# Down projection of a decoder step: second parts a slot later, one bank in two tiles, loads two pairs ahead, one sum by an adding transfer

## The chip, the cores and the metric

The kernel runs on one core of one Trainium2 chip. The metric is the device time of one execution in microseconds, as the median of three runs. Engines are named as in the profile: PE (matrix multiplies, with PEld for its weight loads), DVE (vector work), ACT (copies and activations), POOL, and SP, which issues most of the transfers. A row that ends in "q" (SPq, POOLq) is a transfer being issued by that engine.

## The reference, cut

One layer of a hybrid decoder is computed for 512 prompt rows and 64 sample rows (576 in all), in float32. The change lies in the last stage, the down projection of the gated feed-forward net:

```python
D_MODEL = 2048
D_FF = 5632
def _conv_ffn(x, prev, p):
    u = _rms(x, p['g_ffn']) @ p['w_up']
    up = jnp.concatenate([prev, u], axis=1)
    c = p['conv_b'] + p['conv_w'][CONV_W - 1] * up[:, CONV_W - 1:]
    ...
    a, b = jnp.split(c, 2, axis=-1)
    return x + (jax.nn.silu(a) * b) @ p['w_down'], up[:, T:]
```

So the stage adds `g @ w_down` to `x`, where `g` has 5632 features and the result 2048.

## The kernel before

Float32 operands are split into a first part (`whi`, written by ACT) and a second part (`wlo` = value minus first part, written by DVE), and every product is three passes on PE: first by first, first by second, second by first. The passes come in that order, so a `wlo` is read only in the last third of its product.

The feed-forward's `g` is made tile by tile (44 tiles of 128 features) and kept in device memory as `gd`. The last of the 44 tiles is finished by `convolve(43, i)`, five pieces of DVE and ACT work, before `down` begins.

`down` has two parts. A plain one takes the first 512 of the 5632 features: 16 output tiles `ot`, each 24 matmuls of 128x128 by 288 columns into a `zp` tile, then one DVE addition to the sum `hT`. Then come 40 **pairs** n (5 groups of 1024 features, called chunks here, by 8 pairs of output tiles). A pair is a 2x2 block product done in seven products instead of eight, in the order P1, P6, P5, P7, P2, P3, P4; product number t = 7n + i, and I call the time of product i **slot** i. A product is 12 matmuls (3 passes of 4). It needs weights and activations that are sums of blocks. The weight sums are made per pair: S1 = A21 + A22, S2 = S1 - A11, S3 = A22 - S2, S4 = A12 - S2 (`down_sum`, one DVE operation of 128x512 each). The activation sums T1 to T4 are made once per chunk for the next one (`build`: 13 steps in `todo`, one taken in slot 3 and one in slot 6 of all pairs but the first of a chunk; no steps in the last chunk).

Three banks hold results: P1 and P2 go to `Z[0]`, P6, P7 and P4 to `Z[1]`, P5 and P3 to `Z[2]`. After each product one DVE operation of 128x288 adds its bank to the sums (`down_evict`), and the next product into that bank may start only then.

The order of the work is the order of the code: `down_first(t)` is the ACT copy, `down_second(t)` the DVE difference, `down_product(t)` the matmuls. Before, slot t holds: the first part for t+2, the eviction of t-1, the second part for t+2, a sum if one is due (S3 in slot 0, S4 in slot 2, S1 in slot 4, S2 in slot 5), a step of `todo`, the loads for pair n+1 (slot 1), and product t. Each engine works through its own queue in that order. SP's queue holds the loads (A21 and A22 into two 256 KB tiles of the pool `z` with 8 buffers, A11 and A12 together as one 512 KB tile `raw` with 2 buffers) and, in the last chunk, the stores of y. In the last chunk `store_y` also puts ten PE transposes into each pair, which use the free `fa` banks (4 in all, one of them held as `Z[2]`).

In the trace every instruction has line L189, that of a recording helper, so work is told by its tiles: `hT<-zp` or `hT<-fa` is an eviction, `wlo<-` a second part, `a<-a,a` is S1, `s<-a,raw` S2, `raw<-a,s` S3, `s<-raw,s` S4, and T1 to T4, B11, B21, B22 and `t` belong to `build`. On PE, a product is named by its activations: B11 is P1, T2 is P6, T1 is P5, T3 is P7, B21 is P2, B22 is P3 and T4 is P4.

Of the kernel before, what the change touches and what calls it, by code (L numbers as in the profile page):

```python
# [9 lines left out]
F32 = mybir.dt.float32  # L10
# [3 lines left out]
ALU = mybir.AluOpType  # L14
# [6 lines left out]
HB = 288  # L21
# [257 lines left out]
class Kern:  # L279
# [1910 lines left out]
    def down_weights(self, n, part):  # L2190

        if n >= 40:
            return
        r, c = 512 + 1024 * (n // 8), 256 * (n % 8) + 128 * part
        src = self.w_down[r:r + 1024, c:c + 128].rearrange("(k p) c -> p k c", p=128)
        if part == 0:
            t = self.wpool.tile([128, 8, 128], F32, name="raw", tag="raw", bufs=2)
            self.nc.sync.dma_start(out=t, in_=src)
            self.V[n, "A11"], self.V[n, "A12"] = t[:, :4], t[:, 4:]
        else:  # L2200
            for k in range(2):
                t = self.V[n, f"A2{k + 1}"] = self.vblock(f"a2{k + 1}")
                self.nc.sync.dma_start(out=t, in_=src[:, 4 * k:4 * k + 4])

    def vblock(self, name):
        return self.z(name)[:, :512].rearrange("p (k c) -> p k c", k=4)
# [211 lines left out]
    def finish(self, es, outs, w_down):  # L2418
        nc, a = self.nc, self.a
        self.fpool = self.pool(es, "ffn", side="right")  # L2420
        self.bpool = self.pool(es, "big", side="right")
        self.spawn(self.ffn_consts())
        self.cst, self.ssq, self.W = [None, None], None, {}
        self.B = {name: [[self.operand(name, n, half) for half in range(2)] for n in "hl"]
                  for _, name, _ in self.PRODUCTS.values()}
        order = [o for i in range(8) for o in (i, i + 8)]

        def xload(n):
            if n < 16:
                x = self.z("xr")  # L2430
                nc.sync.dma_start(out=x, in_=self.xT[order[n]])
                return x

        def free(kt):
            if kt == 0:
                self.weights(0, "A11")
                self.weights(0, "A22")
            elif kt in (1, 2):
                self.weights(0, ("A12", "A21")[kt - 1])
            elif kt == 6:  # L2440
                self.U = [self.place(12 + s, (128, FW), "u") for s in range(2)]
                for U in self.U:
                    nc.gpsimd.memset(U[:, 0:2], 0.0)
            elif kt == 7:
                self.C = [self.place(14 + s, (128, FW - 2), "C") for s in range(2)]
                self.first_parts(0, 0)
                self.second_parts()

        def later(kt):
            if kt == 4 and self.rest:  # L2450
                self.rest()
                self.rest = None

        x, self.rest = xload(0), None
        for n, ot in enumerate(order):
            last = n == 15
            ps, = self.gemm([(outs[ot], 128, list(range(8)), self.mixs)],
                            on_kt=lambda kt: (later(kt), last and free(kt)), before=self.mixed)
            nx = xload(n + 1)
            self.out_done(ot, ps, x)  # L2460
            x = nx
        self.rest()
        norm = self.spawn(self.second_norm(), first=True)
        self.Z = [self.zp(), self.zp(), self.ps("fa")]
        self.held.add(self.Z[2].tensor.name)
        self.gs, self.hT = [], {}
        self.gd = self.dram("gd", (128, 44, NT))
        self.st = Stream(self, 2, 4)
        downs = self.add_down(w_down, 0)
        self.w_down = w_down  # L2470
        win = a["win_sample"].rearrange("l b t k g d -> (l b) t (k g d)")
        todo = []
        for f in range(44):
            for i in range(7):
                if f == 0 and i == 3:
                    self.until(lambda: norm.done and not self.threads)
                parts = self.before_slot(f, i)
                if i > 3 and todo:
                    todo.pop(0)()
                self.product(f, i, parts)  # L2480
                if f == 43 and i in (0, 1):
                    todo += self.load_first(i)
            if 2 <= f < 18:
                b, t = (f - 2) // 2, 252 * (f % 2)
                nc.gpsimd.dma_start(out=win[b, t:t + 252],
                                    in_=a["cache_win"][0, b, 8 + t:260 + t].rearrange("t k g d -> t (k g d)"))
        while todo:
            todo.pop(0)()
        self.evict(43, 6)
        for i in range(5):  # L2490
            self.convolve(43, i)
        self.done(self.Z[2])
        self.down(downs)
        self.drain()

    def down(self, downs):
        for ot in range(2):
            self.load_h(ot)
        self.V, self.vs = {}, {}
        Y4 = self.fpool.tile([128, 4, HB], F32, name="Y4", tag="prev")  # L2500
        Y1 = self.fpool.tile([128, HB], F32, name="Y1", tag="cw")
        self.Y = [Y4[:, i] for i in range(4)] + [self.rstd[:, :HB], self.rstd[:, HB:], Y1]
        todo, B = self.build(1)
        for ot in range(16):
            hi, lo = self.st.get(downs[ot])
            o = self.zp()
            for kt in range(4):
                for n, (w, x) in enumerate(((hi, 0), (lo, 0), (hi, 1))):
                    for h in range(2):
                        self.mm(o[:, 512 * h:512 * h + HB], w[:, kt], self.gs[h][x][:, kt],  # L2510
                                kt == 0 and n == 0, kt == 3 and n == 2)
                    if n < 2:
                        self.pump()
            self.st.prep_to(downs[ot] + 5)
            h = self.h2(self.hT[ot])
            self.nc.vector.tensor_tensor(h, self.halves(o), h, ALU.add)
            if ot + 2 < 16:
                self.load_h(ot + 2)
            if 0 < ot < 15:
                todo.pop(0)()  # L2520
            if ot == 11:
                self.down_weights(0, 1)
            elif ot == 13:
                self.down_weights(0, 0)
            elif ot == 14:
                self.down_sum(0, "S1")
                self.down_first(0)
                self.down_sum(0, "S2")
                self.down_second(0)
                self.down_first(1)  # L2530
        self.down_second(1)
        self.Z = [self.zp(), self.zp(), self.ps("fa")]
        self.held.add(self.Z[2].tensor.name)
        for t in range(280):
            n, i = t // 7, t % 7
            if t % 56 == 0 and t:
                B = nextB
            if t % 56 == 0 and t < 224:
                todo, nextB = self.build(2 + t // 56)
            self.down_first(t + 2)  # L2540
            if t:
                self.down_evict(t - 1)
            self.down_second(t + 2)
            for m, name in {0: ((n, "S3"),), 2: ((n, "S4"),), 4: ((n + 1, "S1"),), 5: ((n + 1, "S2"),)}.get(i, ()):
                self.down_sum(m, name)
            if n % 8 and i in (3, 6) and todo:
                todo.pop(0)()
            if i == 1:
                self.down_weights(n + 1, 1)
                self.down_weights(n + 1, 0)  # L2550
            self.down_product(t, B)
        self.down_evict(279)

# [75 lines left out]
```

## Time and profile before

| | |
|---|---|
| median of three runs | 2978.86 us (2977.79 to 2979.95) |
| the profiled execution | 2977.68 us, of which 2975.9 us span |
| PE / DVE / ACT / POOL busy, share of the span | 97% / 75% / 49% / 13% |
| first product of pair 0, first product of pair 33, end | 2435.15, 2884.36, 2975.9 us |
| granted PE clock over the whole run | 0.993 |

The profile is of one execution; stretches are given in microseconds from the span's start. A view called windows gives the busy time of each engine in a stretch, a timeline lists instructions in order, and a view of waits adds up what an engine stood idle for. A granted clock of 1.00 is 2.4 GHz and one of 0.50 is 1.2 GHz. Busy time of DVE counts each operation to its last write, while the next may start some 0.08 us earlier, so durations in a row are a little longer than the distance of two starts.

### The profile page before, as it was taken

What the parts mean: (1) busy time and instruction counts of PE and PEld (TensorE: products, weight loads), DVE (VectorE), ACT (ScalarE), POOL (GpSimd) and SP (SyncE); (2) the same over time, 40 slices, a digit from 0 to 9 for tenths busy, and PEclk for the clock granted to TensorE, in tenths of its full rate; (3) what the DMA queues carried; (4) which work ended last, traced back from release to release, by engine and by line L of the source; (5) the groups of instructions that cost most, each with busy time, mean ns of one, the idle gap of its engine ahead of it and who ended that gap; (6) DMA issues with size and microseconds to landing.
All of it is one profiled execution on the core that took longest, in us unless ns stands there. A gap on an engine that the chain in (4) does not pass through costs nothing.

```text
span 2975.9 us, 56967 instructions
## 1 busy us (share of the span) xinstructions
PE 2880.6 (97%) x21370; PEld 2839.7 (95%) x21370; DVE 2221.1 (75%) x4403; ACT 1459.3 (49%) x2863; POOL 390.3 (13%) x681
## 2 busy tenths in 40 slices
PE   8999999999999999999999999999999998888889
PEld 7999999999999999999999999999999998888889
DVE  4332456766476566468999999999999978888888
ACT  6443568666354555334544454454454534333333
POOL 3011131312301111200111111111110100000000
PEclk9999999999999999999999999999999999999999
DMA  8443333222554566755444543433433452342333
GB/s 246 130 113 82 107 102 89 88 83 78 139 157 126 177 207 220 244 174 176 125 133 124 144 134 110 126 99 109 122 101 109 137 188 81 105 117 79 101 92 109
DMA packets 560143, 385.79 MB, mean 130 GB/s; under 512 B 65477, under 2 KB 527893, under 8 KB 559613
## 3 DMA queue, kind: packets, MB, share of 16 engines
q1 hardware_dynamic: 537068, 308.29, 36.5%
q0 software_dynamic: 22768, 73.86, 7.5%
q8 instruction: 169, 2.77, 0.4%
q14 instruction: 106, 0.86, 0.1%
q10 hardware_dynamic: 32, 0.01, 0.0%
HBM read 316.51 MB, written 75.32 MB: 132 GB/s over the span
## 4 chain that ended last, share of the span: by engine, by line
PE 54%; DVE 10%; issue 5%; ACT 3%; POOL 1%; DMA 0%; ACTq 0%; DVEq 0%; POOLq 0%
PE zp L189 39%; PE fa L189 15%; DVE wlo L189 3%; ACT whi L189 2%; DVE hT L189 1%; DVE s L189 1%; DVE t L189 1%; DVE a L189 1%; DVE raw L189 1%; POOL ret_sample L189 0%; DMA raw<-w_down 0%; DVE B22l L189 0%; POOL mix L189 0%; DVE T2l L189 0%; DVE B11l L189 0%
## 5 line engine op out<-in xcount | busy, mean ns | idle before, releaser
L189 ACT ACTIVATE whi<-raw 128x512 fp32r<-128x512 f32 x588 | 356.0, 625 | 460.7 <-PE zp L189 242.4
L189 DVE TENSOR_TENSOR wlo<-raw,whi 128x512 fp32r<-128x512 f32 x584 | 398.2, 697 | 118.7 <-ACT whi L189 116.1
L189 PE MATMUL zp<-ah,whi 128*128 128x288 f32 (+1 forms) x2208 | 480.9, 299 | 2.1 <-ACT whi L189 1.9
L189 PE MATMUL zp<-al,whi 128*128 128x288 f32 (+1 forms) x2208 | 478.1, 298 | 0.1
L189 PE MATMUL zp<-ah,wlo 128*128 128x288 f32 x2176 | 473.8, 299 | 3.1 <-DVE wlo L189 3.1
L189 ACT ACTIVATE whi<-s 128x512 fp32r<-128x512 f32 x256 | 156.3, 631 | 437.0 <-DVE s L189 343.9
L189 PEld LDWEIGHTS zp<-ah,whi 128*128 128x128 f32 (+1 forms) x2208 | 356.3, 189 | 5.5 <-ACT whi L189 2.3
L189 PEld LDWEIGHTS zp<-ah,wlo 128*128 128x128 f32 x2176 | 351.4, 189 | 6.4 <-DVE wlo L189 3.9
L189 PEld LDWEIGHTS zp<-al,whi 128*128 128x128 f32 (+1 forms) x2208 | 354.7, 188 | 1.8 <-DVE al L189 0.3
L189 ACT ACTIVATE whi<-a 128x512 fp32r<-128x512 f32 x344 | 202.2, 625 | 122.5 <-DVE u L189 78.2
L189 DVE TENSOR_TENSOR wlo<-a,whi 128x512 fp32r<-128x512 f32 x344 | 225.2, 687 | 29.0 <-ACT whi L189 26.2
L189 DVE TENSOR_TENSOR wlo<-s,whi 128x512 fp32r<-128x512 f32 x256 | 168.6, 687 | 28.2 <-ACT whi L189 28.2
L189 PE MATMUL zp<-T2h,whi 128*128 128x288 f32 x576 | 105.3, 301 | 51.5 <-DVE hT L189 51.4
L189 DVE SCALAR_TENSOR_TENSOR C<-u,cw,C 128x592 f32<-128x592 f32 x176 | 146.4, 832 | 3.1
L189 PEld LDWEIGHTS zp<-T2h,whi 128*128 128x128 f32 x576 | 84.4, 189 | 57.6 <-issue 30.5
L189 DVE CUSTOM_DVE_ANT_0 P<-fa,th 128x256 f32<-128x256 f32 (+3 forms) x128 | 60.9, 488 | 63.6 <-PE fa L189 61.7
L189 PE MATMUL zp<-T2h,wlo 128*128 128x288 f32 x576 | 103.4, 301 | 0.0
L189 PE MATMUL zp<-B11h,wlo 128*128 128x288 f32 x576 | 100.6, 294 | 2.3 <-DVE wlo L189 2.3
L189 PE MATMUL zp<-B11h,whi 128*128 128x288 f32 x576 | 100.3, 294 | 1.3 <-ACT whi L189 1.3
L189 DVE TENSOR_TENSOR hT<-zp,hT 128x288 f32<-128x288 f32 (+1 forms) x191 | 90.4, 478 | 14.5 <-PE zp L189 11.8
L189 PE MATMUL zp<-T2l,whi 128*128 128x288 f32 x576 | 101.2, 296 | 0.0
L189 PE MATMUL zp<-B11l,whi 128*128 128x288 f32 x576 | 100.2, 294 | 0.0
(435 smaller groups left out, 6640.1 us busy)
## 6 DMA issues: line engine op xcount, KB each, us to landing
a<-w_up SPq DMA_DIRECT2D x264, 256.0 KB
raw<-w_in SPq DMA_DIRECT2D x102, 512.0 KB
raw<-w_down SPq DMA_DIRECT2D x48, 512.0 KB
raw<-w_up SPq DMA_DIRECT2D x44, 512.0 KB
a<-w_down SPq DMA_DIRECT2D x80, 256.0 KB
raw<-w_out SPq DMA_DIRECT2D x32, 512.0 KB
gd<-g POOLq DMA_DIRECT2D x44, 288.0 KB, 2.9
xr<-xT SPq DMA_DIRECT2D x32, 288.0 KB
```

The costliest lines, as they stand in the source:

```text
L189: return fn(*a, **kw)
```

## The change

Five things change, all in and just before `down`.

1. `convolve(43, i)` moves from before `down` into the first two output tiles of its plain part (pieces 0 and 1 into the first, 2 to 4 into the second). The tiles `Y4` and `Y1`, which reuse memory of the convolution, are allocated after the plain part.
2. The second part is made a slot later: slot t makes it for t+1 instead of t+2. The first part stays two ahead. S2 moves from slot 5 to slot 6 and stands first there.
3. S1 is no DVE operation any more: A21 is loaded as before, and POOL issues a transfer that reads A22 from device memory and adds it to the tile of A21. A22 is still loaded by itself, too.
4. The weights of pair n+2 instead of n+1 are loaded, `raw` in slot 5 and the two others in slot 6.
5. `Z[1]` alternates between a `zp` tile and an `fa` tile from pair to pair. Two of the four `fa` banks are held then.

```diff
             for k in range(2):
                 t = self.V[n, f"A2{k + 1}"] = self.vblock(f"a2{k + 1}")
                 self.nc.sync.dma_start(out=t, in_=src[:, 4 * k:4 * k + 4])
+            t = self.V[n, "S1"] = self.V[n, "A21"]
+            self.nc.gpsimd.dma_start(out=t, in_=src[:, 4:], accum_op=ALU.add)
...
         self.evict(43, 6)
-        for i in range(5):
-            self.convolve(43, i)
...
             self.st.prep_to(downs[ot] + 5)
+            for i in ((0, 1), (2, 3, 4))[ot] if ot < 2 else ():
+                self.convolve(43, i)
...
-            if ot == 11:
-                self.down_weights(0, 1)
-            elif ot == 13:
-                self.down_weights(0, 0)
-            elif ot == 14:
-                self.down_sum(0, "S1")
-                self.down_first(0)
-                self.down_sum(0, "S2")
-                self.down_second(0)
-                self.down_first(1)
-        self.down_second(1)
-        self.Z = [self.zp(), self.zp(), self.ps("fa")]
-        self.held.add(self.Z[2].tensor.name)
+            if ot in (11, 12):
+                self.down_weights(ot - 11, 1)
+            elif ot in (13, 14):
+                self.down_weights(ot - 13, 0)
...
+        self.down_sum(0, "S2")
+        for t in range(2):
+            self.down_first(t)
+        self.down_second(0)
+        A, C = self.zp(), self.ps("fa")
+        self.held.add(C.tensor.name)
+        bs = self.zp(), self.ps("fa")
+        self.held.add(bs[1].tensor.name)
         for t in range(280):
...
+            if i == 6:
+                self.down_sum(n + 1, "S2")
             self.down_first(t + 2)
             if t:
                 self.down_evict(t - 1)
-            self.down_second(t + 2)
-            for m, name in {0: ((n, "S3"),), 2: ((n, "S4"),), 4: ((n + 1, "S1"),), 5: ((n + 1, "S2"),)}.get(i, ()):
+            if i == 0:
+                self.Z = [A, bs[n % 2], C]
+            self.down_second(t + 1)
+            for m, name in {0: ((n, "S3"),), 2: ((n, "S4"),)}.get(i, ()):
                 self.down_sum(m, name)
...
-            if i == 1:
-                self.down_weights(n + 1, 1)
-                self.down_weights(n + 1, 0)
+            if i == 5:
+                self.down_weights(n + 2, 0)
+            elif i == 6:
+                self.down_weights(n + 2, 1)
             self.down_product(t, B)
```

**DVE at the end of a pair.** These are DVE's rows from slot 4 of one pair to slot 0 of the next, in the first chunk, before:

```order
L189 TENSOR_TENSOR a_31324<-a_31324,a_31326 128x512
L189 TENSOR_TENSOR hT<-zp,hT 128x288
L189 TENSOR_TENSOR wlo<-raw,whi 128x512
L189 TENSOR_TENSOR s_31404<-a_31324,raw 128x512
L189 TENSOR_TENSOR hT<-fa,hT 128x288
L189 TENSOR_TENSOR wlo<-s_31404,whi 128x512
L189 TENSOR_TENSOR T2l<-t,T2h 128x576
L189 TENSOR_TENSOR t<-B21l,t 128x576
L189 TENSOR_TENSOR hT<-zp,hT 128x288
L189 TENSOR_TENSOR wlo<-a_31324,whi 128x512
L189 TENSOR_TENSOR raw<-a_31326,s_31404 128x512
```

And these are the rows of the changed kernel from slot 5 of that pair to slot 0 of the next one:

```order
L189 TENSOR_TENSOR hT<-zp,hT 128x288
L189 TENSOR_TENSOR wlo<-a_31155,whi 128x512
L189 TENSOR_TENSOR s_31417<-a_31290,raw 128x512
L189 TENSOR_TENSOR hT<-fa,hT 128x288
L189 TENSOR_TENSOR wlo<-raw,whi 128x512
L189 TENSOR_TENSOR T2l<-t,T2h 128x576
L189 TENSOR_TENSOR t<-B21l,t 128x576
L189 TENSOR_TENSOR hT<-zp,hT 128x288
L189 TENSOR_TENSOR wlo<-s_31417,whi 128x512
L189 TENSOR_TENSOR raw<-a_31292,s_31417 128x512
```

The row of S1 is gone, S2 stands in slot 6 ahead of the eviction of P3, and the second part that follows the same eviction is that of the product one earlier.

**PE's banks.** In one pair of two, P6, P7 and P4 write an `fa` tile; this is the difference at such a pair:

```order
 L189 MATMUL zp<-B11h,wlo 128x288 x4
-L189 MATMUL zp<-T2h,whi 128x288 x4
-L189 MATMUL zp<-T2l,whi 128x288 x4
-L189 MATMUL zp<-T2h,wlo 128x288 x4
+L189 MATMUL fa<-T2h,whi 128x288 x4
+L189 MATMUL fa<-T2l,whi 128x288 x4
+L189 MATMUL fa<-T2h,wlo 128x288 x4
 L189 MATMUL fa<-T1h,whi 128x288 x4
 L189 MATMUL fa<-T1l,whi 128x288 x4
 L189 MATMUL fa<-T1h,wlo 128x288 x4
```

The order of the products is unchanged; what P6 waits for is now the eviction of the P4 before last.

**DVE at the start of the pairs.** This is the difference after the last step of `build` in the plain part; the second row that stays is the addition of the last output tile:

```order
 L189 TENSOR_TENSOR B22l<-B22l,B22h 128x1152
-L189 TENSOR_TENSOR a_30885<-a_30885,a_30887 128x512
-L189 TENSOR_TENSOR s_30980<-a_30885,raw 128x512
-L189 TENSOR_TENSOR wlo<-raw,whi 128x512
 L189 TENSOR_TENSOR hT<-zp,hT 128x576
-L189 TENSOR_TENSOR wlo<-s_30980,whi 128x512
+L189 TENSOR_TENSOR s_31011<-a_30883,raw 128x512
+L189 TENSOR_TENSOR wlo<-raw,whi 128x512
+L189 TENSOR_TENSOR wlo<-s_31011,whi 128x512
```

S2 and the first second part of pair 0 now stand behind that addition.

## Rows read from the trace of the kernel before

**Rows 1.** Page, part 1: busy time and share of each engine.
```profile
PE 2880.6 (97%) x21370; PEld 2839.7 (95%) x21370; DVE 2221.1 (75%) x4403; ACT 1459.3 (49%) x2863; POOL 390.3 (13%) x681
```

**Rows 2.** Windows: length, busy PE, PEld, DVE, ACT, POOL, clock, DMA share, GB/s.
```profile
2435.00:2884.00 449.00, 389.70 (x2773) 380.27 (x2772) 377.87 (x676) 168.79 (x283) 0.00 (x0) 0.97 0.35 101
2884.00:2970.00 86.00, 86.00 (x665) 85.85 (x664) 75.78 (x157) 34.13 (x63) 0.00 (x0) 1.00 0.38 110
```

**Rows 3.** Waits from 2435 to 2884: us in total, times, longest.
```profile
DVE wlo L189 <- ACT whi L189: 63.6, 126, 1.6
PE zp L189 <- DVE hT L189: 57.9, 39, 2.6
```

**Rows 4.** Timeline of PE: first products of pairs 0, 17, 18, 33, 35, 36.
```profile
2435.15 0.69 PE L189 MATMUL zp<-B11h,whi 128*128 128x288 f32 x4
...
2666.49 0.69 PE L189 MATMUL zp<-B11h,whi 128*128 128x288 f32 x4
...
2677.59 0.69 PE L189 MATMUL zp<-B11h,whi 128*128 128x288 f32 x4
...
2884.36 0.69 PE L189 MATMUL zp<-B11h,whi 128*128 128x288 f32 x4
...
2908.77 0.69 PE L189 MATMUL zp<-B11h,whi 128*128 128x288 f32 x4
...
2920.98 0.69 PE L189 MATMUL zp<-B11h,whi 128*128 128x288 f32 x4
```

**Rows 5.** Timeline of DVE at the end of pair 5, then PE.
```profile
2515.68 0.69 DVE L189 TENSOR_TENSOR a<-a,a 128x512 f32<-128x512 f32 x1
2516.29 0.45 DVE L189 TENSOR_TENSOR hT<-zp,hT 128x288 f32<-128x288 f32 x1
2516.65 0.69 DVE L189 TENSOR_TENSOR wlo<-raw,whi 128x512 fp32r<-128x512 f32 x1
...
2518.72 0.69 DVE L189 TENSOR_TENSOR wlo<-s,whi 128x512 fp32r<-128x512 f32 x1 [0.41 <-ACT whi L189]
2519.33 0.75 DVE L189 TENSOR_TENSOR T2l<-t,T2h 128x576 fp32r<-128x576 f32 x1
2520.11 0.76 DVE L189 TENSOR_TENSOR t<-B21l,t 128x576 f32<-128x576 f32 x1
2520.79 0.45 DVE L189 TENSOR_TENSOR hT<-zp,hT 128x288 f32<-128x288 f32 x1
...
2521.39 0.37 PE L189 MATMUL zp<-T2h,whi 128*128 128x288 f32 x1 [2.60 <-DVE hT L189]
```

**Rows 6.** Windows behind another wait of PE, columns as above.
```profile
2574.00:2576.50 2.50, 2.50 (x13) 2.50 (x12) 2.09 (x5) 1.15 (x2) 0.00 (x0) 0.50 0.36 105
```

**Rows 7.** Timeline at the start of the plain part: DVE, then PE.
```profile
2382.20 3.31 DVE L189 SCALAR_TENSOR_TENSOR C<-u,cw,C 128x592 f32<-128x592 f32 x4
...
2387.09 0.40 PE L189 MATMUL zp<-B11h,wlo 128*128 128x288 f32 x1 [2.34 <-DVE wlo L189]
```

**Rows 8.** Timeline of DVE: the addition of the last output tile.
```profile
2436.03 0.75 DVE L189 TENSOR_TENSOR hT<-zp,hT 128x576 f32<-128x576 f32 x1
```

**Rows 9.** A load of A21: SP's timeline; windows of its bytes, and of A22 with `raw`.
```profile
2559.64 5.49 SPq L189 DMA_DIRECT2D a<-w_down  x2
...
2560.50:2562.00 1.50, 1.50 (x13) 1.50 (x12) 1.09 (x4) 0.98 (x2) 0.00 (x0) 1.00 0.59 174
2565.50:2569.00 3.50, 3.50 (x28) 3.50 (x28) 2.60 (x6) 1.66 (x3) 0.00 (x0) 1.00 0.81 229
```

**Rows 10.** Page, part 6: transfers issued by POOL: count, KB, us to landing.
```profile
al<-mix POOLq DMA_DIRECT2D x8, 288.0 KB, 4.8
xc<-xc POOLq DMA_DIRECT2D x4, 256.0 KB, 6.5
```

**Rows 11.** Timeline of DVE and POOL at the end of the stage before.
```profile
2375.25 1.35 DVE L189 TENSOR_TENSOR B11l<-B11l,B11h 128x1152 fp32r<-128x1152 f32 x1
2375.63 0.55 POOL L189 DMA_DIRECT2D gd<-g  x1 [4.19 <-DVE g L189]
2376.18 1.69 POOL L189 COPY u<-prev 128x16 f32<-128x16 f32 x1
```

More of the change, by code (lines that the diff above doesn't have):

```diff
@@ L2499, in down @@
         self.V, self.vs = {}, {}
-        Y4 = self.fpool.tile([128, 4, HB], F32, name="Y4", tag="prev")
-        Y1 = self.fpool.tile([128, HB], F32, name="Y1", tag="cw")
-        self.Y = [Y4[:, i] for i in range(4)] + [self.rstd[:, :HB], self.rstd[:, HB:], Y1]
         todo, B = self.build(1)
@@ L2520, in down @@
                 todo.pop(0)()
-            if ot == 11:
-                self.down_weights(0, 1)
-            elif ot == 13:
-                self.down_weights(0, 0)
-            elif ot == 14:
-                self.down_sum(0, "S1")
-                self.down_first(0)
-                self.down_sum(0, "S2")
-                self.down_second(0)
-                self.down_first(1)
-        self.down_second(1)
-        self.Z = [self.zp(), self.zp(), self.ps("fa")]
-        self.held.add(self.Z[2].tensor.name)
+            if ot in (11, 12):
+                self.down_weights(ot - 11, 1)
+            elif ot in (13, 14):
+                self.down_weights(ot - 13, 0)
+        Y4 = self.fpool.tile([128, 4, HB], F32, name="Y4", tag="prev")
+        Y1 = self.fpool.tile([128, HB], F32, name="Y1", tag="cw")
+        self.Y = [Y4[:, i] for i in range(4)] + [self.rstd[:, :HB], self.rstd[:, HB:], Y1]
+        self.down_sum(0, "S2")
[6 more added lines that the diff above has]
+        self.held.add(bs[1].tensor.name)
         for t in range(280):
@@ L2537, in down @@
                 B = nextB
-            if t % 56 == 0 and t < 224:
-                todo, nextB = self.build(2 + t // 56)
+            if i == 6:
+                self.down_sum(n + 1, "S2")
             self.down_first(t + 2)
@@ L2542, in down @@
                 self.down_evict(t - 1)
-            self.down_second(t + 2)
-            for m, name in {0: ((n, "S3"),), 2: ((n, "S4"),), 4: ((n + 1, "S1"),), 5: ((n + 1, "S2"),)}.get(i, ()):
+            if i == 0:
+                self.Z = [A, bs[n % 2], C]
+            self.down_second(t + 1)
+            for m, name in {0: ((n, "S3"),), 2: ((n, "S4"),)}.get(i, ()):
                 self.down_sum(m, name)
+            if t % 56 == 0 and t < 224:
+                todo, nextB = self.build(2 + t // 56)
             if n % 8 and i in (3, 6) and todo:
                 todo.pop(0)()
-            if i == 1:
-                self.down_weights(n + 1, 1)
-                self.down_weights(n + 1, 0)
+            if i == 5:
+                self.down_weights(n + 2, 0)
+            elif i == 6:
+                self.down_weights(n + 2, 1)
             self.down_product(t, B)
```

## The prediction

> **What bounds the kernel now.** I read four views in this order. The page says PE is busy 97% of the span [rows 1], so a gain can only come from a stretch where PE waits or runs slowly. The windows find it: from 2435 to 2884, pairs 0 to 32, PE is busy 389.7 of 449 us at a mean clock of 0.97, and from 2884 on it never waits [rows 2]. PE's timeline gives the floor: pair 17 takes 2677.59 - 2666.49 = 11.10 us without a wait, 1.586 us per slot, while the 33 pairs up to 2884.36 take 449.2 us, 13.61 each [rows 4]. At 11.10 they would take 366.3. So **82.9 us** is all there is to win in them. The later pairs take 12.21 [rows 4], the same floor plus the transposes of the stores, with no wait.
>
> The view of waits says who costs it: PE waits 57.9 us, 39 times, for an eviction by DVE [rows 3]. The other 25 us follow from these waits: behind a long one the granted clock stands at 0.50, 1.2 GHz instead of 2.4 [rows 6] (3% of 449 is 13 us of lost work), and the other 12 are refilling, 0.3 behind each of 39 waits. DVE itself loses 63.6 us waiting for ACT's first parts [rows 3].
>
> The timeline at the end of pair 5 shows one such wait being made [rows 5]. DVE runs S1, an eviction and a second part back to back, idles 0.41 for ACT because it wants the second part of S2's product in the very slot in which ACT makes the first, then does two steps of `build`, and only then evicts P4. P6 of the next pair wants that bank and waits 2.60.
>
> **DVE's load, step by step.** Distances of starts [rows 5]: a sum or a second part 0.61 (2515.68 to 2516.29), an eviction 0.36 (2516.29 to 2516.65), a build piece 0.68 to 0.78; a large one is bounded by its 1.35 [rows 11]. Per pair before: 7 second parts + 4 sums = 11 x 0.61, plus 7 x 0.36 = 9.2. Building a chunk's sums is 16 small pieces and 3 large, 16 x 0.68 + 3 x 1.35 = 14.9, over 8 pairs 1.9. The waits for ACT are 63.6 / 33 = 1.9. Together 13.0 of the 13.6 measured, so DVE sets the pace of these pairs.
>
> Edit by edit:
>
> - S1 off DVE: 9.2 - 0.6 = 8.6 per pair.
> - Second part a slot later: its first part is then a slot old. ACT is 38% busy there (168.8 of 449, [rows 2]), so it has it ready and I put the 1.9 at nothing. It ends nearer to its use: made in slot t, read in the last third of slot t+1, that is 1.586 + 1.06 = 2.65 us after the slot's start.
> - Together DVE needs 8.6 + 1.9 = **10.5 per pair against PE's 11.1**: PE becomes the bound, with DVE 95% loaded.
> - Two tiles for one bank: P6 no longer depends on the last eviction of the pair before. P7 still needs P6's, which has one slot between; that is the closest dependence left.
>
> An average of 95% can still hide waits, so the worst stretch slot by slot. A slot without extras is 0.36 + 0.61 = 0.97; one with a sum 1.58; slots 3 and 6 may add two build pieces, 1.46. In slot 6 that makes 0.61 + 0.97 + 1.46 = 3.04, so DVE enters slot 0 late by 3.04 - 1.59 = 1.45. Slot 0 (S3) takes 1.58 and keeps it; slot 1 takes 0.97, 0.83 late; slot 2 (S4) 0.82; slot 3 with two more pieces 2.43, 1.66 late; slot 4 1.04, slot 5 0.42, and a second slot 6 of this kind leaves it 1.87 late. What is bearable: a second part ends at lateness + 0.36 + 0.69 (its duration), so up to about 1.5 it costs nothing; P6's eviction in slot 2 may be late by about 1.0 and is by 0.82. Only 1.66 and 1.87 are over, by 0.2 and 0.4. Slots of this kind follow each other in two pairs of eight, and the large pieces end a chunk, so I count three waits of 0.2 to 0.4 in a chunk, each with 0.3 to refill: 1.5 to 2 us, I take 1.5, **+6 us** in four chunks. From below it is 0 (S2 can start before its slot where DVE is early). From above, one wait of 0.6 with its refill in each of the 28 pairs with build work: 25.
>
> **The adding transfer.** POOL does nothing in this stretch [rows 2], so nothing is queued behind its wait for the A21 load; the one who would wait is S2, and behind it on DVE the eviction and the second part of that slot. No row shows an adding transfer, so I look for the time it may take. The load of pair n+2 starts when `raw` is free, after the second part of P2 in slot 3, about 1.4 us into it. On SP, A21 and A22 now stand behind `raw`, and the y stores behind them; SP's issues per pair are the same three. 768 KB landed between 2565.5 and 2569, 3.5 us, and the first bytes come 1.1 us after an issue (2559.64, 2560.5, [rows 9]): A21 is there about 5 us after `raw`'s issue. S2 of that pair stands in slot 6 of the next one, ten slots or 15.9 us after slot 3 began. Left for POOL's issue and landing, L: 15.9 - 1.4 - 5 - 0.2 = **9.3 us**. Nearest rows: 288 KB from memory to a tile 4.8, 256 KB at the slowest 6.5 [rows 10]. The second read, of the destination, is at most another load of 256 KB, 1.5 us [rows 9]. So L is 4.8 to 8; I take 6.3, hidden with 3 us to spare, cost **0**. A pair is the larger of 11.1 and 0.7 x (L + 6.6).
>
> **The ends of the stage.** The convolution's four long DVE pieces (3.31 us) stand ahead of the second parts that the plain part needs, and PE waits 2.34 us for them [rows 7]. Spread behind two output tiles they stand behind these: **-2.3** (0 if the pieces merely move the wait). At the other end S2 and the second part of product 0 now stand behind the last addition, which starts at 2436.03 [rows 8]: 0.68 (a build piece has its size) + 0.61 + 0.69 later is 2438.0, less the 0.6 by which the addition was itself behind S1, S2 and a second part, 2437.4. The last third of product 0 wants it at 2435.15 + 1.06 = 2436.2: **+1.2** (0 to 2). `Y4` and `Y1` allocated later cost nothing; ACT's first write to them is in slot 1. The pairs from 33 on stay at 12.2: DVE loses work there too, but PE never waited. Two free `fa` banks instead of three could make a transpose wait for a copy of y, up to 0.6 in 7 pairs: 0 to 4, I take 0.
>
> **Sum.** -82.9 + 6 + 0 - 2.3 + 1.2 = -78.0 us. Against the profiled run, 2977.68 - 78.0 = 2899.7; that run lies 1.2 under the median, so the forecast is 2978.9 - 78.0 = **2901**, a ratio of 0.974.
>
> **Rivals.**
>
> *DVE's waits stay* (12%). If DVE goes on losing 1.9 us per pair, now for PE's ends or for ACT's steps of `build`, it needs 10.5 + 1.9 = 12.4, and the gain is 33 x (13.61 - 12.4) = 40: 2978.9 - 40 - 1.1 = 2938. For it: these waits are the second largest item [rows 3], and light slots can't be worked ahead, since an eviction waits for PE. Against it: nothing DVE reads from ACT is younger than a slot any more. Half of the waits give 2915.
>
> *POOL and DVE hold each other up* (4%). A copy of 128x16 on POOL took 1.69 us beside DVE's two-input operations, but a transfer issued by POOL inside such an operation took 0.55 [rows 11]. If the adding transfer's issue behaved like the copy, one per pair would cost DVE up to 0.7 of its 0.6 to spare: 11.2 per pair, 33 x 0.1 = 3 us, and up to 0.5 per pair, 16 us, if each such hold makes DVE miss a slot: 2904 to 2917. The Trainium skill ("SBUF — State Buffer", "Who interferes with whom") states that a DVE instruction with two SBUF inputs contends with a GpSimd instruction that reads SBUF, and that descriptor generation needs only the write side, which it marks as inferred; by its first half the time would be these 2904 to 2917, by its second the forecast. The trace agrees with the second half where a plain transfer is issued.
>
> *The adding transfer is late, and the kernel slower than before* (8%, 1% of it no change). By the formula above each microsecond of L over 9.3 adds 0.7 per pair. The gain is gone where a pair takes 13.4 on average over all 40, at L = 12.5, twice the slowest row. At L = 15 a pair takes 15.1 and the time is 2978.9 + 40 x 15.1 - 534.7 - 1.1 = **3047** (534.7 is what the 40 pairs take now). For it: no row shows this operation; it moves 512-byte rows and reads what it writes. Against it: it would have to be two to three times slower than any transfer of its size here.
>
> **How the numbers follow.** The forecast holds 76%: 2891 (no lateness: -6; no cost in product 0: -1.2; the refill at the convolution saved too: -0.3; and 2 for the spread of the median's own runs) to 2914 (the upper half of the lateness, +9, with the fa banks' 4). The first rival holds 12%, half of it under 2925; the second lies inside. The range 2891 to 2925 leaves out the rest of the first rival and the slow one. A measurement of this kernel tells 0.2%, 6 us, from no change; faster by more than that are the forecast and the first two rivals, 92%; in between lies only a transfer with L near 12.5, 1%; slower 7%.
>
> **What would show it.** Right: pairs 0 to 32 at 11.1 to 11.3, clock 1.00 from 2435 on, PE's waits for evictions of `hT` under 10 us, DVE's waits for ACT under 20, S2 never waiting for a transfer, 2.3 less before the plain part's second tile, one new wait of about 1.2 in product 0. Wrong: S2 (`s<-a,raw`) with a DMA as what ended its idle time; a P7 that waits in every pair; transposes that wait for `fa` in the last chunk.

## The result, and the profile after

| | before | after |
|---|---|---|
| median | 2979.4 us (four runs, 2977.8 to 2983.7) | 2901.1 us (four runs, 2900.0 to 2906.7) |
| ratio | | 0.9739, 95% interval 0.9722 to 0.9756 |
| the profiled execution, span | 2977.68, 2975.9 us | 2900.03, 2898.3 us |

The forecast was 2901. The sum came out by more than it deserved: one term had the wrong sign, one was some five times too large, and one was missing. The page after, part 1, against [rows 1]:

```profile
PE 2858.4 (99%) x21370; PEld 2824.4 (97%) x21370; DVE 2188.8 (76%) x4363; ACT 1459.4 (50%) x2863; POOL 442.9 (15%) x721
```

The windows of pairs 0 to 32 and of the last pairs (busy PE, PEld, DVE, ACT, POOL, clock, DMA share, GB/s), against [rows 2]:

```profile
2435.80:2806.14 370.34, 368.20 (x2775) 366.89 (x2774) 349.43 (x643) 168.95 (x284) 41.13 (x32) 1.00 0.61 142
2806.14:2892.00 85.86, 85.77 (x660) 85.05 (x659) 73.03 (x152) 34.09 (x61) 7.72 (x6) 1.00 0.57 133
```

PE now works 368.2 of 370.3 us at a clock of 1.00, where it worked 389.7 of 449 at 0.97, and DVE stands at 94%. The first products of pairs 0, 18, 19 and 33, against [rows 4], give the pace: pair 18 takes 2648.79 - 2637.68 = 11.11 us, the 33 pairs 370.34, or 11.22 each.

```profile
2435.80 0.69 PE L189 MATMUL zp<-B11h,whi 128*128 128x288 f32 x4
...
2637.68 0.69 PE L189 MATMUL zp<-B11h,whi 128*128 128x288 f32 x4
2648.79 0.69 PE L189 MATMUL zp<-B11h,whi 128*128 128x288 f32 x4
...
2806.14 0.43 PE L189 MATMUL zp<-B11h,whi 128*128 128x288 f32 x2
```

The waits from 2440 to 2800 (us in total, times, longest) are the answer to [rows 3]: no row of a `wlo` that waits for ACT, where 63.6 us stood, and none of PE waiting for an eviction, where 57.9 stood. A row is new: S2 waits for the adding transfer, three times.

```profile
DVE hT L189 <- PE zp L189: 12.3, 28, 0.9
DVE s L189 <- DMA a<-w_down: 4.7, 3, 2.4
DVE hT L189 <- PE fa L189: 3.0, 6, 0.9
...
PE zp L189 <- DVE wlo L189: 1.0, 1, 1.0
```

DVE's timeline at the end of pair 5 answers [rows 5]. The five operations of slot 6 follow each other without the 0.41 us for ACT, and the last row is the eviction of P4, 1.04 us into the next pair (which starts at 2503.72). Before, P6 stood waiting for exactly this eviction; now it writes the other tile.

```profile
2501.71 0.68 DVE L189 TENSOR_TENSOR s<-a,raw 128x512 f32<-128x512 f32 x1
2502.33 0.46 DVE L189 TENSOR_TENSOR hT<-fa,hT 128x288 f32<-128x288 f32 x1
2502.70 0.68 DVE L189 TENSOR_TENSOR wlo<-raw,whi 128x512 fp32r<-128x512 f32 x1
2503.30 0.75 DVE L189 TENSOR_TENSOR T2l<-t,T2h 128x576 fp32r<-128x576 f32 x1
2504.09 0.76 DVE L189 TENSOR_TENSOR t<-B21l,t 128x576 f32<-128x576 f32 x1
2504.76 0.45 DVE L189 TENSOR_TENSOR hT<-fa,hT 128x288 f32<-128x288 f32 x1
```

Where the time went, by the two profiled executions:

| stretch | before | after | difference | forecast |
|---|---|---|---|---|
| up to the plain part's first product | 2381.13 | 2378.86 | -2.27 | 0 |
| plain part, up to pair 0 | 54.02 | 56.94 | +2.92 | -2.3 |
| pairs 0 to 32 | 449.21 | 370.34 | -78.87 | -75.7 |
| pair 33 to the end of the span | 91.54 | 92.16 | +0.62 | 0 |
| sum | 2975.9 | 2898.3 | -77.6 | -78.0 |

The first line is no effect of the change: the code up to there is the same in all kernels of this document, and in their profiles that point lies between 2377.9 and 2382.8. So a stretch is read from its own start, and medians that differ by less than 2 us say little here.

### The profile page after: what moved, and what is told of

Same layout as the page of the kernel before. It is cut to its first block, busy times and chain, and to the rows that moved or that the text cites. A ratio compares the mean times of both kernels' runs of the same rounds, so it can differ in the third digit from the quotient of the medians.

```text
span 2898.3 us, 56858 instructions
## 1 busy us (share of the span) xinstructions
PE 2858.4 (99%) x21370; PEld 2824.4 (97%) x21370; DVE 2188.8 (76%) x4363; ACT 1459.4 (50%) x2863; POOL 442.9 (15%) x721
## 4 chain that ended last, share of the span: by engine, by line
PE 63%; issue 4%; DVE 3%; DMA 1%; POOL 1%; ACT 0%; POOLq 0%; SPq 0%; ACTq 0%; DVEq 0%
PE zp L189 43%; PE fa L189 20%; DVE wlo L189 1%; DMA a<-w_down 1%; DVE hT L189 0%; DVE s L189 0%; POOL ret_sample L189 0%; DMA S<-state_ret 0%; POOL mix L189 0%; DVE t L189 0%; DVE raw L189 0%; DMA al<-mix 0%; DMA raw<-w_down 0%; DVE P L189 0%; DVE kd L189 0%
## 5 line engine op out<-in xcount | busy, mean ns | idle before, releaser
L189 POOL DMA_DIRECT2D a<-w_down x40 | 51.5, 1289 | 416.6 <-DVE raw L189 68.0
L189 POOL COPY u<-prev 128x16 f32<-128x16 f32 x88 | 30.4, 345 | 453.7 <-DVE C L189 428.1
L189 PEld LDWEIGHTS zp<-B11h,whi 128*128 128x128 f32 x576 | 85.2, 189 | 3.3 <-ACT C L189 3.3
L189 PEld LDWEIGHTS zp<-B11h,wlo 128*128 128x128 f32 x576 | 84.9, 189 | 2.8 <-DVE wlo L189 2.8
L189 DVE TENSOR_TENSOR s<-a,raw 128x512 f32<-128x512 f32 x128 | 84.0, 684 | 4.7 <-DMA a<-w_down 4.7
```

Of the source, the lines that this page charges most:

```text
L189: return fn(*a, **kw)
```

## Three parts, in all combinations

Theory: DVE's load sets the pace. A pair takes the larger of PE's 11.1 us and DVE's load, which S1 raises by 0.6 and the waits for ACT by 1.9; the second tile carries no load. Rival: the chain through one bank, P4's eviction before P6, is the whole cost, and the second tile alone removed it. The three parts were undone one at a time, then two at a time; all else stays as in the changed kernel.

**S1 on DVE again.**

```diff
-            t = self.V[n, "S1"] = self.V[n, "A21"]
-            self.nc.gpsimd.dma_start(out=t, in_=src[:, 4:], accum_op=ALU.add)
...
-            for m, name in {0: ((n, "S3"),), 2: ((n, "S4"),)}.get(i, ()):
+            for m, name in {0: ((n, "S3"),), 2: ((n, "S4"),), 4: ((n + 1, "S1"),)}.get(i, ()):
```

> The changed kernel with S1 on DVE again (in slot 4; no adding transfer). DVE-load theory (a pair takes the larger of PE's 11.1 us and DVE's load, 10.5 with all parts): the load becomes 11.1, equal to PE's, so a late slot is no longer caught up; 0.2 to 0.5 us in each of 33 pairs, 2908 to 2918. Bank-chain rival (only the wait of P6 for the eviction of P4 cost time, and the second tile removed it): at most 5 more, 2901 to 2906.

Measured: 2905.8 (ratio to before 0.9754, 0.9738 to 0.9770). That is in the rival's range and under the load theory's; this run alone would have spoken for the rival. The window of 2440 to 2800 shows DVE busy for 98% of it, and PE still for 357.2 of 360:

```profile
2440.00:2800.00 360.00, 357.22 (x2675) 353.91 (x2674) 352.02 (x649) 162.90 (x273) 0.00 (x0) 1.00 0.41 117
```

So an engine beside PE may be full to 98% and cost 5 us in 33 pairs, if what it does next hardly waits for a third engine (1.3 us for ACT in this window).

**The second part in the slot of its first part.**

```diff
-            if i == 6:
-                self.down_sum(n + 1, "S2")
...
-            self.down_second(t + 1)
+            self.down_second(t + 2)
-            for m, name in {0: ((n, "S3"),), 2: ((n, "S4"),)}.get(i, ()):
+            for m, name in {0: ((n, "S3"),), 2: ((n, "S4"),), 5: ((n + 1, "S2"),)}.get(i, ()):
```

> The changed kernel with the second part made again in the slot of its first part (for t+2, S2 back in slot 5). DVE-load theory: DVE again loses 1.9 us per pair waiting for ACT, its load is 12.4, 33 pairs at 1.3 more are 43: 2940 (2930 to 2945), with some 60 us of DVE waits for ACT between the first product and pair 33. Bank-chain rival: the waits for ACT end before a bank is needed, at most 10 more: 2901 to 2911.

Measured: 2951.7 (0.9910, 0.9894 to 0.9927), 50.6 more than the changed kernel; the load theory's number was too low. Waits and window of 2440 to 2800:

```profile
DVE wlo L189 <- ACT whi L189: 57.0, 113, 1.6
...
PEld fa L189 <- ACT whi L189: 26.5, 20, 1.6
PEld zp L189 <- ACT whi L189: 20.7, 14, 1.6
PE zp L189 <- DVE hT L189: 17.9, 14, 1.4
...
2440.00:2800.00 360.00, 319.98 (x2359) 312.77 (x2358) 302.18 (x543) 143.06 (x241) 35.98 (x28) 1.00 0.53 124
```

DVE is busy 302 us, less than in the kernel with S1, and PE loses 40. DVE's work and its waits for ACT fill the window (302.2 + 57.0 of 360), so DVE still sets the pace: pairs 0 to 32 take 424.6 us in this profile, 12.87 each, of which some 10.8 are work and 2.0 waits. The waits go round in a ring: DVE waits for ACT's first part, so the next sum and the next step of `build` come late, ACT waits for these, and PE, which needs both, waits for banks and for ACT's first parts (the two PEld rows).

S2 changed its place too, and this run doesn't separate that. But the waits don't stand at the sums alone: 21.6 of the 57.0 us stand before second parts of S1 and A22, which no operation of DVE makes.

```profile
L189 DVE TENSOR_TENSOR wlo<-a,whi 128x512 fp32r<-128x512 f32 x56 | 38.5, 688 | 21.6 <-ACT whi L189 21.6
```

**One tile for Z[1].**

```diff
-        bs = self.zp(), self.ps("fa")
-        self.held.add(bs[1].tensor.name)
+        bs = (self.zp(),) * 2
```

> The changed kernel with one tile for Z[1] in all pairs. DVE-load theory: the load stays 10.5, P6 finds its bank late only in the pairs with two more build pieces in slot 6, by 0.2 us and 0.3 of refilling: 2 to 6 more, 2903 to 2907. Bank-chain rival: the 57.9 us of waits for evictions come back with 0.7 to 1 of their cost: 2941 to 2961.

Measured: 2903.7 (0.9747, 0.9731 to 0.9763). As the load theory had it; the rival's 40 us are not there.

**Only the second tile, only the adding transfer, only the later second part** (two of the three diffs above each).

> The changed kernel with S1 on DVE and the second part in the slot of its first part: of the three parts in the pairs only the second tile is left. DVE-load theory: load 13.0, 1.9 more than 11.1 in 33 pairs is 63: 2964 (2955 to 2975). Bank-chain rival: nearly the whole gain stays, 2901 to 2916.

> The changed kernel with the second part in the slot of its first part and one tile for Z[1]: of the three parts in the pairs only the adding transfer is left. DVE-load theory: 10.5 + 1.9 = 12.4 per pair, and the run without the later second part alone gave 2951.7; one tile costs little more, 2952 to 2960. Bank-chain rival: without the second tile the old waits come back whole, 2970 to 2979.

> The changed kernel with S1 on DVE and one tile for Z[1]: of the three parts in the pairs only the later second part is left. If the parts add up: 2901.1 + 4.7 (S1 on DVE) + 2.5 (one tile) = 2908. DVE-load theory: load 11.1 leaves no slack, and a late eviction of P4 now meets P6 at once, so more than the sum: 2910 to 2920. Bank-chain rival: 2941 or more.

Measured, with the others, as the change against before:

| second tile | adding transfer | later second part | median, us | ratio (95%) |
|---|---|---|---|---|
| x | | | 2973.3 | 0.9982 (0.9972 to 0.9991) |
| | x | | 2955.2 | 0.9921 (0.9905 to 0.9938) |
| | | x | 2911.0 | 0.9772 (0.9756 to 0.9789) |
| x | x | | 2951.7 | 0.9910 (0.9894 to 0.9927) |
| x | | x | 2905.8 | 0.9754 (0.9738 to 0.9770) |
| | x | x | 2903.7 | 0.9747 (0.9731 to 0.9763) |
| x | x | x | 2901.1 | 0.9739 (0.9722 to 0.9756) |

The eighth combination, none of the three with the other edits in place, was not run; the kernel before stands for it, so each row also holds what the other edits do. Against it the later second part alone gives 68 of the 78 us, the adding transfer alone 23, the second tile alone 5 to 6; in pairs 0 to 32 of the profiles alone it is 68.6, 23.8 and 4.7 us of 78.9. They don't add up, since PE's 11.1 is a floor: once the second part is late, the transfer is worth 5 to 7 and the tile 3 to 5. All three single parts fell into the load theory's ranges, and the bank-chain rival has fallen: with the second tile alone PE still waits 32.1 us for evictions from 2440 to 2800, since DVE lacks the time.

## Is it the age of the first part?

A later second part also stands nearer to its use and behind other evictions. To tell these apart, the second part was put back two slots ahead, and ACT's first part made three ahead, so that DVE again finds it a slot old.

```diff
-            if i == 6:
-                self.down_sum(n + 1, "S2")
-            self.down_first(t + 2)
+            for m, name in {0: ((n, "S3"),), 2: ((n, "S4"),), 5: ((n + 1, "S2"),)}.get(i, ()):
+                self.down_sum(m, name)
+            self.down_first(t + 3)
...
-            self.down_second(t + 1)
-            for m, name in {0: ((n, "S3"),), 2: ((n, "S4"),)}.get(i, ()):
-                self.down_sum(m, name)
+            self.down_second(t + 2)
```

> The changed kernel with the second part back in slot t for t+2, as in the run that cost 50.6 us, but the first part made one more slot ahead (for t+3), so that it is again a slot old; S2, S3 and S4 move ahead of the first part and of the eviction in slots 5, 0 and 2, S2 a slot earlier. If the gain of the later second part is that DVE wants no first part younger than a slot: DVE's waits for ACT between 2440 and 2800 fall from 57 to under 10 us; the sums ahead of the evictions and S2 nearer to the adding transfer cost up to 8, 2901 to 2909. Rival, that the gain is the shorter time between second part and use (whatever the age of the first part): 2940 to 2952.

Measured: 2899.3 (0.9727, 0.9711 to 0.9744), no slower than the changed kernel and just under the range of the first theory. The sums ahead of the evictions are not quite free: pairs 0 to 32 take 371.9 us in this profile, 1.5 more than in the changed kernel, though S2's waits for its transfer lengthen no pair here. The row of a `wlo` that waits for ACT is gone from the waits of 2440 to 2800, and PE is busy as in the changed kernel:

```profile
ACT whi L189 <- DVE s L189: 76.0, 58, 2.6
...
DVE s L189 <- DMA a<-w_down: 2.3, 3, 0.9
...
PE fa L189 <- DVE hT L189: 1.6, 4, 0.4
...
2440.00:2800.00 360.00, 358.34 (x2694) 356.45 (x2693) 338.79 (x625) 169.51 (x276) 41.11 (x32) 1.00 0.61 140
```

So the cause is the age of the first part when DVE wants it: two ways to make it a slot old both take DVE's waits away, and PE's with them. It does not hold for every engine. In this run ACT wants S2, S3 and S4 in the very slot in which DVE makes them and waits 76.0 us for S2 and S4, and in the changed kernel, where it wants S2 so (slot 6), 112.4 us; in neither does PE wait for ACT, which is busy less than half of the time (169.5 of 360). What must not wait for a part of the same slot is the engine without time to spare, here DVE.

## The adding transfer

The page of the changed kernel, part 6 (KB each, us to landing), and one pair's issue on POOL between DVE's operations:

```profile
a<-w_down POOLq DMA_DIRECT2D x40, 256.0 KB, 4.4
...
2459.54 0.75 DVE L189 TENSOR_TENSOR T3l<-t,T3h 128x576 fp32r<-128x576 f32 x1
2459.89 1.27 POOL L189 DMA_DIRECT2D a<-w_down  x1 [9.18 <-DVE t L189]
2460.21 0.45 DVE L189 TENSOR_TENSOR hT<-fa,hT 128x288 f32<-128x288 f32 x1
2460.58 0.68 DVE L189 TENSOR_TENSOR wlo<-s,whi 128x512 fp32r<-128x512 f32 x1
```

The page counts landing from the start of the issue, so the 1.3 us of the issue lie inside the 4.4: L is 4.4 us, against the 6.3 taken and the 9.3 allowed. DVE's operations beside the issue last as long as elsewhere, so the rival in which POOL and DVE hold each other up did not come. By the Trainium skill ("SBUF — State Buffer", "Who interferes with whom") a DVE instruction with two SBUF inputs contends with POOL's reads, and making descriptors needs the write interface, which is marked there as inferred. This trace agrees with that inference: the issues of pairs 0 to 32 took 1.27 to 1.30 us, in a stretch where DVE is 94% busy. An issue that fell into 8.18 us in which DVE stood still took 1.31 (at 2449.08, in the run with the loads one pair ahead, below), so DVE's work does not lengthen it.

**What adding costs.** The same transfer without `accum_op`:

```diff
-            self.nc.gpsimd.dma_start(out=t, in_=src[:, 4:], accum_op=ALU.add)
+            self.nc.gpsimd.dma_start(out=t, in_=src[:, 4:])
```

> The changed kernel with POOL's transfer not adding but only writing A22 over A21 (the sum A21 + A22 is left out). If adding is what makes the transfer dear: issue back from 1.28 us to the 0.55 of POOL's other transfers, landing from 4.4 to about 3, and S2 waits for it no more at the start of chunks. If its 512-byte rows are: issue 1.28 and landing 4.4 as before, and the time stays 2901.

Measured, in one execution: 2898.0, and S2 never waits. The page's part 6 and an issue:

```profile
a<-w_down POOLq DMA_DIRECT2D x40, 256.0 KB, 3.2
...
2459.08 0.75 POOL L189 DMA_DIRECT2D a<-w_down  x1 [10.43 <-DVE t L189]
```

Adding costs 1.2 of the 4.4 us, 0.5 of them in the issue. The 0.75 that is left lies over the 0.55 of [rows 11], which the expectation had; why is not shown.

**Where it is late.** At the start of a chunk SP also issues the four loads for the next sums. The rows for the sums of pair 25, from the issue of its loads (SP, POOL, DVE, PE):

```profile
2699.98 0.37 SPq L189 DMA_DIRECT2D raw<-w_down  x1
2700.39 3.41 SPq L189 DMA_DIRECT2D a<-w_down  x2
...
2707.58 1.28 POOL L189 DMA_DIRECT2D a<-w_down  x1 [12.06 <-DVE raw L189]
...
2716.04 0.69 DVE L189 TENSOR_TENSOR s<-a,raw 128x512 f32<-128x512 f32 x1 [2.38 <-DMA a<-w_down]
...
2717.75 0.80 PE L189 MATMUL zp<-B11h,wlo 128*128 128x288 f32 x4 [0.95 <-DVE wlo L189]
```

POOL starts 7.6 us after the issue of `raw` (I had put 5 for A21's landing; the row names S3, which ended at 2707.56, as what came last, so A21 was there somewhat earlier) and S2 gets its sum 8.5 us after that, 16.1 in all against the 14.3 that were allowed; S2 waits 2.4, and pair 25 takes 12.33 us. S2 waits so in pairs 9, 17 and 25; pair 9 bears it, pairs 17 and 25 lose 1.6 us together. This is the slower rival's mechanism, in 3 of 40 pairs.

**How much the loads two ahead are worth.** Loads one pair ahead in slot 1, as before, with the adding transfer kept (the plain part then loads pair 0 alone, and not pair 1):

```diff
-            if i == 5:
-                self.down_weights(n + 2, 0)
-            elif i == 6:
-                self.down_weights(n + 2, 1)
+            if i == 1:
+                self.down_weights(n + 1, 1)
+                self.down_weights(n + 1, 0)
```

> The changed kernel with the weights loaded one pair ahead in slot 1, as in the kernel before, and the adding transfer kept. A21 is issued 1.6 us into the pair, lands 2.5 later, POOL takes 1.3 to issue and 4.4 to land: 9.8 us into the pair, where S2 is due at 9.5. Theory that the loads two ahead carry nothing in most pairs (lateness under 1 us is borne): 2901 to 2911. Rival, the late-transfer case: the two loads and the 512 KB of the pair stretch the adding transfer to the 8.4 us seen at the start of a chunk, S2 is 3 us late in each pair and a pair takes 12.5 to 14: 2950 to 3010.

Measured: 2919.9 (0.9799, 0.9782 to 0.9815), between both. The ordinary pairs stay at 11.1, as the first theory has it. Its 9.8 us into the pair counted the issue twice; with the 5.2 us from issue to landing on this run's page it is 9.3, inside the 9.5. The 19 us lie at the ends, in the rows below (SP, POOL and DVE for S2 of pair 1, then SP and DVE in pair 35). The loads for pair 1 stand right behind the four that `build` issues in pair 0, POOL gets A21 8.2 us after its issue, the adding transfer takes another 8, and pair 1 lasts 19.3 us. And in the last chunk SP issues the loads only behind the stores of y, so that the pairs take 13 to 14.6 instead of 12.2.

```profile
2440.22 0.58 SPq L189 DMA_DIRECT2D B21l<-gd  x1
2440.91 1.81 SPq L189 DMA_DIRECT2D a<-w_down  x2
...
2449.08 1.31 POOL L189 DMA_DIRECT2D a<-w_down  x1 [22.96 <-DMA a<-w_down]
...
2457.28 0.69 DVE L189 TENSOR_TENSOR s<-a,raw 128x512 f32<-128x512 f32 x1 [8.18 <-DMA a<-w_down]
...
2849.07 0.47 SPq L189 DMA_DIRECT2D y_sample<-yd  x1
2849.65 1.08 SPq L189 DMA_DIRECT2D a<-w_down  x2
...
2859.17 0.69 DVE L189 TENSOR_TENSOR s<-a,raw 128x512 f32<-128x512 f32 x1 [2.26 <-DMA a<-w_down]
```

## The convolution, and a faster version

The forecast had -2.3 for the move of the convolution. The rows at its new place (ACT, DVE, PE) show a new wait of 3.08 us:

```profile
2384.51 0.63 ACT L189 ACTIVATE whi<-raw 128x512 fp32r<-128x512 f32 x1 [5.88 <-DMA raw<-w_down]
2385.05 1.64 ACT L189 ACTIVATE C<-u,cw 128x592 f32<-128x592 f32 x2
...
2385.95 1.71 DVE L189 SCALAR_TENSOR_TENSOR C<-u,cw,C 128x592 f32<-128x592 f32 x2 [4.14 <-ACT C L189]
2387.57 0.75 DVE L189 TENSOR_TENSOR hT<-zp,hT 128x576 f32<-128x576 f32 x1
...
2388.47 0.58 PE L189 MATMUL zp<-B11h,whi 128*128 128x288 f32 x1 [3.08 <-ACT C L189]
```

Read from the top: ACT's first part waits 5.88 us for its load. The convolution's copies are now behind it on ACT, its DVE pieces wait for these, and behind them on DVE stands the addition of the first output tile, whose bank the third tile needs. The last row names ACT; but ACT's copies ended at 2386.69, and PE starts right after that addition's end, at 2388.32. The granted clock was 0.77 from 2380 to 2395.

**The convolution before the plain part again.**

```diff
-            for i in ((0, 1), (2, 3, 4))[ot] if ot < 2 else ():
-                self.convolve(43, i)
...
+        for i in range(5):
+            self.convolve(43, i)
         self.V, self.vs = {}, {}
```

> The changed kernel with the five pieces of the convolution before the plain part again. By the prediction's term (-2.3 for the move): 2.3 slower, 2903.4. By the trace of the changed kernel, where the copies of the convolution stand on ACT behind a first part that waits for its load, DVE's addition behind them and PE's third output tile behind that (3.08 us): from the first product of the plain part to that of pair 0 it takes 54.0 again instead of 56.9, so 2898.2.

Measured: 2900.8 (0.9736, 0.9720 to 0.9752), the same as the changed kernel within 0.3 us, so neither expectation. The old wait is back, at 2.34 us:

```profile
2388.44 0.61 PE L189 MATMUL zp<-B11h,wlo 128*128 128x288 f32 x1 [2.34 <-DVE wlo L189]
```

The plain part takes 55.2 us in this profile (the clock was 0.89 behind the wait), and 54.0 before; with the moved pieces 54.7 to 56.9 in ten profiles. One wait has taken the place of another; which place is better by a microsecond stays open.

**Taking it apart.** ACT's two copies ahead of the plain part, DVE's pieces behind the additions of the first three tiles:

```diff
+        for s in range(2):
+            self.tap(43, s)
...
+        late = [lambda: self.taps(43, 0), lambda: (self.convolve(43, 2), self.taps(43, 1)), lambda: self.gate(43)]
...
             self.nc.vector.tensor_tensor(h, self.halves(o), h, ALU.add)
+            if late:
+                late.pop(0)()
```

> Only (a) of the run before: the ACT copies of the convolution ahead of the plain part, its DVE pieces behind the additions. If what DVE and ACT queue ahead of the first tiles is the cause of both the old wait of 2.34 us and the new one of 3.08: no wait over 0.5 on PE from 2380 to 2395, 2897.5. If the loads of the first weights are the cause whatever the order: a wait of 2 to 3 us stays and the time is 2901.

Measured: 2895.5 (0.9721, 0.9706 to 0.9736). PE doesn't wait in the plain part, which takes 51.0 us: both waits came from the order in the queues of ACT and DVE, not from the loads. The median is 2 us under the expectation, which is about what medians can tell here.

**All that was found, mended.** To this come S2 and the parts of pair 0 ahead of the last addition, and the chunk's loads spread over two pairs:

```diff
+            if ot == 14:
+                self.down_sum(0, "S2")
+                self.down_first(0)
+                self.down_second(0)
+                self.down_first(1)
...
+            if i == 4 and n % 8 == 7 and n < 31:
+                self.build(3 + n // 8, early=True)
```

Here `early` allocates and loads B11 and T1 alone, and the next call of `build` takes them over.

> A version to beat the changed kernel. (a) The two ACT copies of the convolution before the plain part, its DVE pieces behind the additions of the first three output tiles; (b) S2, both first parts and the second part of pair 0 ahead of the addition of the last output tile; (c) of the four loads for a chunk's sums, the two for B11 and T1 one pair earlier. If the trace of the changed kernel is read rightly: (a) first product of the plain part to that of pair 0 in 51.5 to 52.5 us instead of 55 to 57; (b) pair 0 in 11.1 instead of 12.38; (c) pairs 17, 25 and 32 without S2 waiting for the adding transfer, 2.0 us. Together 7 us: 2894 (2892 to 2896). Rival, that each wait only moves (S2 of pair 0 then holds back the addition of the last tile; the early loads meet the transfers of the pair before): 2899 to 2902.

Measured: 2892.5 (0.9707, 0.9694 to 0.9720), 8.6 less than the changed kernel. In its windows, of pairs 0 to 32 and of the plain part, PE is busy all but 0.1 us:

```profile
2429.42:2796.88 367.46, 367.38 (x2774) 366.76 (x2773) 348.73 (x642) 168.67 (x284) 41.11 (x32) 1.00 0.62 143
2378.42:2429.42 51.00, 51.00 (x389) 51.00 (x387) 40.41 (x59) 20.57 (x32) 6.71 (x11) 1.00 0.71 210
```

## Why the prediction was right, and where it was not

- **The floor and the 82.9 us.** Right: 11.10 to 11.11 us in the ordinary pairs, clock 1.00. PE waits for no eviction there.
- **DVE's load.** Right: the waits for ACT were the largest item, and DVE's work and waits together set the pace. Both terms were a little small. Without the later second part the kernel loses 50.6 us (54.3 in pairs 0 to 32 of the profile, 1.6 per pair), though 12.4 - 11.1 is 1.3: DVE's work was 10.8 and not 10.5, its waits 2.0 and not 1.9.
- **Half of DVE's waits.** The 2915 given for them doesn't follow from the rival's own numbers: 2978.9 - 33 x (13.61 - 11.45) - 1.1 is 2906.5. No other term hangs on it.
- **Residual lateness, +6.** Mis-sized; it measured about 1. In the version without other waits the 33 pairs take 367.46, 1.2 over the floor, 0.14 of it in each of four pairs that end a chunk and 0.36 in pair 32. The slot-by-slot sum let S2 begin with its slot; in the trace it began 0.4 us earlier (2501.71, its slot at 2503.72 - 1.59 = 2502.13), so DVE entered slot 0 1.04 late and not 1.45. The text named this as the reason for the lower bound 0, and took a value too far from it.
- **S2 never waiting for a transfer.** Wrong at the start of chunks, +1.6. The step that failed took the time to A21's landing, 5 us, and the bytes beside it from an ordinary pair; the four loads of `build` in the same 12 us were not asked about. 768 KB was not all that the transfers had to carry there.
- **The adding transfer, 0, with L = 6.3.** Right in all but those pairs: L was 4.4. The break-even of 12.5 was far; the slowest in a profile of the changed kernel was 9.5.
- **Product 0, +1.2.** Right: pair 0 takes 12.38, 1.28 over the floor. It is shown by the version that mends it, where it takes 11.10.
- **The convolution, -2.3.** Wrong; +2.9 in the profiled run, nothing in the medians. The term looked at the queue the pieces left (DVE's second parts) and not at the two they joined: ACT's, behind a first part that waits for a load, and DVE's, ahead of an addition.
- **From pair 33 on, 0.** Mis-sized by 0.6: the term said that PE never waits there, and in pair 33, which takes 12.78 instead of 12.21, it does. DVE stands 1.61 us at the second of that pair's two copies of y, and PE's weight loads then wait 0.19 and 0.32 us for second parts, each with some refill. With one tile that pair took 12.61, so a bank too few isn't the cause. The rows, of DVE and of PEld:

```profile
2810.28 0.28 DVE L189 COPY yd<-fa 64x128 f32<-64x128 f32 x1 [1.61 <-DMA y_prompt<-yt]
...
2815.11 0.57 PEld L189 LDWEIGHTS zp<-B21h,wlo 128*128 128x128 f32 x4 [0.32 <-DVE wlo L189]
```

- **Sum.** The errors were -5 (lateness), +1.6 (S2), +5.2 (convolution), +0.6 (pair 33) and -2.3 (ahead of the change). That they cancel is luck, and the narrow hit says nothing for the terms.

## What to carry to other kernels

When two engines that work in order feed each other, count the age of each operand in slots: where the fuller engine wants a part in the slot in which the other makes it, both come late, and the third engine waits for both; the emptier engine may wait so without cost. A slot of distance was worth more here than the operation taken off the busy engine. A piece of work that is moved must be looked up in every queue that it joins, not in the one that it leaves, and a transfer's time must be taken from the stretch in which it will run, with all that is issued there. Terms of a sum are checked one by one, from the start of their own stretch, since a right total can hide two wrong ones.

## What the runs showed of the hardware

- An adding transfer of 256 KB landed 4.4 us after the start of its issue, 1.28 of them the issue itself; the same without adding took 3.2, with 0.75 for the issue. Beside four loads of 576 KB the adding one took 8.4 to 9.5.
- DVE at 98% of its time beside PE cost 5 us in 33 pairs, while DVE at 84% (302 of 360) with waits for ACT cost 50: the busy share did not tell which was the worse.
- The granted clock was not the same behind like waits of PE. Behind the wait of 2.34 us it stayed at 1.00 (2.4 GHz) in the kernel before, and fell to 0.50 (1.2 GHz) with the convolution put back; PE had been busy without a break ahead of both. The windows right behind the two waits, in that order:

```profile
2387.10:2390.00 2.90, 2.90 (x22) 2.90 (x23) 1.81 (x3) 0.00 (x0) 0.17 (x1) 1.00 0.74 228
...
2388.50:2391.40 2.90, 2.90 (x12) 2.90 (x13) 1.75 (x3) 0.00 (x0) 0.12 (x1) 0.50 0.76 236
```
